# mLSTM values as seven products of halves ahead of the convolutions, with weight sums made by adding DMAs

## The chip, the cores and the metric

The kernel runs on one core of a Trainium2 chip. The metric is the device time of one execution in microseconds (us), the median of several runs; lower is better.

## What is computed

One decoder block on 512 tokens of width 1024. A normalised input `hN` (512 x 1024) is multiplied by one wide matrix whose columns are cut into the inputs of two branches. Branch A is an mLSTM with 4 heads of width 256, branch B a native sparse attention. The outputs of the branches are projected, weighted by the gates `g_a` and `g_b`, added, projected once more, added to `x` and normalised.

```python
hN = _rmsnorm(x, norm_g[l])
p = _split_in(hN @ w_in[l])
mq = jax.nn.silu(_causal_dwconv(p["m_q"], conv_q_w[l], conv_q_b[l]))
mk = jax.nn.silu(_causal_dwconv(p["m_k"], conv_k_w[l], conv_k_b[l]))
mh = _mlstm(mq, mk, p["m_v"], p["m_i"] + b_igate[l], p["m_f"] + b_fgate[l])
mh = _head_layernorm(mh, mh_norm_g[l]).astype(x.dtype)
ya = jax.nn.sigmoid(p["m_o"]) * mh * jax.nn.silu(p["m_z"])
...
yb = yn * jax.nn.silu(p["n_z"])
merged = (jax.nn.sigmoid(p["g_a"]) * (ya @ w_branch_a[l])
          + jax.nn.sigmoid(p["g_b"]) * (yb @ w_branch_b[l]))
x = x + merged @ w_out[l]
```

The part in question is `p["m_v"] = hN @ w_in[:, 2048:3072]`, the values of the mLSTM: 512 tokens by 1024 columns, summed over 1024.

## The kernel before

**Precision.** Each f32 operand is split in a high part, rounded to a shorter format, and a low part, the rest. A product of two f32 blocks takes three matmuls: high by high, high by low, low by high. The transposed input lies in `hTh` and `hTl` (128 partitions, 8 blocks of the summed dimension, 512 tokens). `weights(src)` (lines 155 to 161) fetches 512 KB of weights into `wr` by a DMA issued on SP, copies them to `wh` on ACT and subtracts on DVE to get `wl`; `split` (line 144) does both; every ACT, DVE and POOL operation of the kernel is recorded at line 93, inside a wrapper.

**The stream of jobs.** Weight products are jobs of one queue, `Stream`. A job has a `load` (its call of `weights`) and a generator that issues one matmul at each step. The stream keeps two jobs loaded ahead of the running one. Matmuls of the attention and of the mLSTM heads are written into the program between steps of the stream (`stream.step(6)` and the like), so that TensorE (PE) has projection work while a softmax or a normalisation runs on other engines. The program's order fixes the order on each engine; engines run in order and wait for each other through semaphores.

**Kinds of jobs.** A `cols` job makes 128 columns for all 512 tokens: 8 blocks x 3 passes = 24 matmuls of 128x512 into a PSUM bank `pp`. Its `post` follows on ACT and DVE: for a convolution (`conv`) one ACT operation and three DVE operations for the four taps, a tanh, a product, and a split into `qkh` and `qkl`; for a merge gate one tanh into a tile `s`.

**Order after the attention.** When the attention has ended (its pools are given back), the stream holds: `convs(0)` (4 jobs), `values(0)` (4 jobs), convolutions of head 1, values of the other half, convolutions of heads 2 and 3, and eight gate jobs between and behind them. The first 8 of these jobs, `convs(0)` and `values(0)`, run at once (`stream.run(8)`), and then the loop over four heads begins: each head makes a decay matrix from `ghl` and `sel`, multiplies queries by keys (`qkh`, `qkl`), multiplies by the values (`yah`, `yal`), normalises, and takes steps of the stream between these. `values(half)` (lines 1095 to 1128) makes 512 of the 1024 value columns in four quarters of the summed dimension; a quarter has 4 token blocks x 2 blocks of the sum x 3 passes = 24 matmuls of 128x512, on the banks `ps` and `pt`.

**The tail.** Behind the heads come the six remaining gate jobs, for each of eight blocks of columns a product with `w_branch_a` (24 matmuls) and one with `w_branch_b` (12), and the last projection, which is already done in seven products of halves (Strassen's algorithm) with the tiles `T`, `m11` and `mx2`.

Of the kernel before, what the change touches and what calls it, by code (L numbers as in the profile page):

```python
# [26 lines left out]
START_FILL = 12  # L27
LAG = 3
EARLY = 2
AHEAD = 8  # L30
NORM_FILL = 30

MQ, MK, MV, MO, MZ, MI = 0, 1024, 2048, 3072, 4096, 5120
# [44 lines left out]
def build(  # L78
# [39 lines left out]
    def f(ap):  # L118
        return ap.bitcast(F32)
# [55 lines left out]
    class Stream:  # L175
# [45 lines left out]
    def cols(c0, post, parts=1):  # L221
        def gen(w):
            ps = PP()
            n = T // parts
            for i in range(parts):
                ts = slice(i * n, i * n + n)
                yield from passes(
                    ps[:, ts], lambda k: w[0][:, k, :], lambda k: w[1][:, k, :],
                    lambda k: hTh[:, k, ts], lambda k: hTl[:, k, ts], ND,
                )  # L230
                if i < parts - 1:
                    yield
            post(ps)

        stream.add(lambda: wcols(c0), gen)
# [334 lines left out]

    def gate_ab(base, j, pl):
        def post(ps):
            s = pl.tile([128, T], F32, name="s", tag="s", bufs=EARLY if pl is ybp else AHEAD)
            A(s, ps, AF.Tanh, scale=0.5)
            halves[base, j] = s

        cols(base + j * 128, post)
# [485 lines left out]
        pool.memset(f(vals(h)[:, :, 256:257]), 1.0)  # L1063
        pool.memset(f(vals(h)[:, :, 257:258]), 0.0)

    sgp = ctx.enter_context(tc.tile_pool(name="sgp", bufs=4))
    mlp = tc.tile_pool(name="ml", bufs=1)
    mp = mlp.__enter__()
    later_only = cst[:, CDM : CDM + 128].unsqueeze(1).broadcast_to([128, NT, 128])
    qk, done = {}, set()  # L1070

# [20 lines left out]

        cols((MQ, MK)[i] + (h * 2 + e) * 128, post)

    def values(half):
        banks = []

        def gen(q):
            def run(w):
                if q == 0:  # L1100
                    banks.extend((PS(), PT(), PS(), PT()))
                for tb in range(NT):
                    ts = slice(tb * 128, tb * 128 + 128)
                    ps = banks[tb]
                    for j in range(2):
                        k = 2 * q + j
                        a, b = hTh[:, k, ts], hTl[:, k, ts]
                        pe.matmul(ps, a, w[0][:, j], start=k == 0, stop=False)  # L1108
                        yield
                        pe.matmul(ps, a, w[1][:, j], start=False, stop=False)  # L1110
                        yield
                        pe.matmul(ps, b, w[0][:, j], start=False, stop=k == ND - 1)  # L1112
                        if j == 0:
                            yield
                    if q == 3:
                        hs = slice(2 * half, 2 * half + 2)
                        hi = yah[:, hs, tb * 258 : tb * 258 + 256]
                        lo = yal.rearrange("p (h e) t -> p h (e t)", h=4)
                        lo = lo[:, hs, tb * 256 : tb * 256 + 256]
                        split(ps.rearrange("p (h d) -> p h d", h=2), hi, lo)  # L1120
                    if tb < NT - 1:
                        yield

            return run

        c0 = MV + half * 512
        for q in range(4):
            stream.add(lambda q=q: weights(wv[:, 2 * q : 2 * q + 2, c0 : c0 + 512]), gen(q))

    later = [(base, j) for j in range(ND) for base in (GA, GB)][EARLY:]  # L1130
    ahead = deque(later[:AHEAD])

    def gates_ahead(n):
        for _ in range(n):
            gate_ab(*ahead.popleft(), sgp)
# [12 lines left out]
    gates_ahead(1)  # L1148
    convs(2)
    values(1)  # L1150
    convs(3)
    gates_ahead(4)
    stream.run(8)

    for h in range(4):
        (qh, ql), (kh, kl) = qk[0, h], qk[1, h]
# [72 lines left out]
        while h < 3 and h + 1 not in done:  # L1229
            stream.step(1)  # L1230
        if h < 3:
            stream.run((1, 4, 1)[h])

    mlp.__exit__(None, None, None)
    gtp.__exit__(None, None, None)
# [1 line left out]
    with tc.tile_pool(name="fin", bufs=1) as fp:  # L1237
# [10 lines left out]
        wbv = w_branch_b[0].rearrange("(k p) c -> p k c", p=128)  # L1248
        wov = w_out[0].rearrange("(k p) c -> p k c", p=128)
        L, R = slice(0, 512), slice(512, D)  # L1250

# [21 lines left out]

        def gate_into(base, j, dst):
            halves[base, j] = dst
            cols(base + j * 128, lambda ps: A(dst, ps, AF.Tanh, scale=0.5))
# [15 lines left out]
        def branch(base, j, yh, yl, nk):  # L1292
            def gen(w):
                o = 0 if nk == ND else (j % 2) * 128
                ps = PP()
                yield from passes(
                    ps, lambda k: w[0][:, k, o : o + 128], lambda k: w[1][:, k, o : o + 128],
                    yh, lambda k: yl[:, k], nk,
                )
                s = halves[base, j]  # L1300
                dve.scalar_tensor_tensor(s, s, 1.0, ps, OP.add, OP.mult)
                if base == GB:
                    t = halves.pop((GA, j))
                    dve.tensor_tensor(t, t, halves.pop((GB, j)), OP.add)
                    if j < 4:
                        split(t[:, :256], m11[0][:, j], m11[1][:, j])
                    else:
                        split(t, mx2[0][:, j - 4], mx2[1][:, j - 4])
                    me[j] = t
                    if j > 3:  # L1310
                        sums(j - 4)

            def load():
                if nk == ND:
                    return weights(wav[:, :, j * 128 : j * 128 + 128])
                if j % 2 == 0:
                    halves["w"] = weights(wbv[:, :, j * 128 : j * 128 + 256])
                return halves["w"]

            stream.add(load, gen)  # L1320

        for i, (base, j) in enumerate(later[AHEAD:]):
            gate_into(base, j, fp.tile([128, T], F32, name="g", tag="g", bufs=6))
            if i in (1, 3):
                combine(i // 2)
        for j in range(ND):
            branch(GA, j, ya, yal, ND)
            branch(GB, j, lambda k: ybh[:, k], ybl, 4)

        xo, fg = {}, {}  # L1330

        def fetch_x():
            for hf in (1, 0):
                hs = slice(hf * 512, hf * 512 + 512)
                for tb in range(NT):
                    t = sgp.tile([128, 512], F32, name="s", tag="s", bufs=AHEAD)
# [130 lines left out]
        def after5(l):  # L1467
            partway(2 + l, Z()[l], 1)
# [114 lines left out]
```

## Time and profile before

| what | value |
|---|---|
| median of 3 runs | 628.36 us (628.16 to 628.82) |
| span of the profiled execution, first to last instruction | 626.6 us |
| median above that span | 1.7 us |
| matmuls on PE | 3057 |
| weight loads into PE (PEld), busy | 82% |
| ScalarE (ACT), busy | 50% |
| GpSimd (POOL), busy | 12% |
| data moved by DMA | 60.79 MB, mean 97 GB/s |

The profile records one execution; its time outside the span is not recorded, so the difference to the median stands for it. How to read it: a matmul of 128x512 is listed with a length of 0.39 us, but matmuls are pipelined, and the next one starts 0.23 us later. The pitch, from start to start, is what one matmul costs. An engine's busy share says little by itself; where an engine waits, and for whom, is in the views that list the waits.

### The profile page before, as it was taken

Reading aid. Unit: us, or ns where it says so; the run is one execution under the profiler, and the core shown is the slowest. Engines: PE = TensorE matmul, PEld = TensorE weight load, DVE = VectorE, ACT = ScalarE, POOL = GpSimd, SP = SyncE. Lnnn points to the kernel's source line nnn. Section 1 sums busy time; section 2 is a strip of 40 time slices with the busy share of each in tenths; the row PEclk is TensorE's granted clock in tenths of the full one; section 3 lists DMA queues with packets and bytes.
Section 4 is the critical chain, followed back from the end, with each engine's and each line's share of the span. In section 5 each row is a group of like instructions: output and inputs, shape, how many; then the busy total and the mean of one; then the engine's idle time right before and its main releaser. Section 6 shows DMA issues by size and latency. Waiting matters only on the chain.

```text
span 626.6 us, 8445 instructions
## 1 busy us (share of the span) xinstructions
PE 614.9 (98%) x3057; PEld 512.4 (82%) x3057; DVE 428.7 (68%) x838; ACT 314.1 (50%) x605; POOL 76.4 (12%) x159
## 2 busy tenths in 40 slices
PE   8999999999999999999999999999999999999995
PEld 6988888888788888778888888888888888888884
DVE  4877776876866856758468868656875624578985
ACT  5675556556556656545354554344553232234654
POOL 6220012212221321300000000000000000000013
PEclk9999999999999999999999999999999999999998
DMA  8647532212221122123322322331422752333403
GB/s 284 173 113 186 133 85 67 69 43 59 69 68 51 51 69 67 35 71 98 102 67 68 100 68 69 100 101 33 101 68 67 236 167 86 101 117 101 167 35 134
DMA packets 88602, 60.79 MB, mean 97 GB/s; under 512 B 2881, under 2 KB 79845, under 8 KB 88561
## 3 DMA queue, kind: packets, MB, share of 16 engines
q1 hardware_dynamic: 87982, 59.21, 33.1%
q10 hardware_dynamic: 578, 1.05, 0.5%
q8 instruction: 24, 0.39, 0.3%
q14 instruction: 18, 0.14, 0.1%
HBM read 57.10 MB, written 2.10 MB: 94 GB/s over the span
## 4 chain that ended last, share of the span: by engine, by line
PE 53%; DVE 2%; POOL 1%; ACT 1%; issue 1%; ACTq 0%; DVEq 0%; POOLq 0%
PE pp L213 12%; PE pp L217 12%; PE pp L215 12%; PE pt L1110 1%; PE ps L1110 1%; PE pt L1108 1%; PE ps L1112 1%; PE ps L1108 1%; PE pt L1112 1%; DVE s L93 1%; PE ps L173 1%; PE ps L172 1%; PE ps L171 1%; PE pt L1197 1%; PE pt L1195 1%; PE pt L1196 1%
## 5 line engine op out<-in xcount | busy, mean ns | idle before, releaser
L213 PE MATMUL pp<-hTh,wh 128*128 128x512 f32 (+1 forms) x488 | 191.8, 393 | 0.0
L215 PE MATMUL pp<-hTl,wh 128*128 128x512 f32 (+1 forms) x488 | 191.1, 391 | 0.0
L217 PE MATMUL pp<-hTh,wl 128*128 128x512 f32 (+1 forms) x488 | 190.6, 391 | 0.0
L93 DVE TENSOR_TENSOR wl<-wr,wh 128x1024 fp32r<-128x1024 f32 x86 | 106.0, 1235 | 59.5 <-ACT wh L93 58.4
L93 ACT ACTIVATE wh<-wr 128x1024 fp32r<-128x1024 f32 x86 | 90.9, 1058 | 83.7 <-PE pp L215 52.5
L217 PEld LDWEIGHTS pp<-hTh,wl 128*128 128x128 f32 x488 | 91.9, 188 | 16.6
L213 PEld LDWEIGHTS pp<-hTh,wh 128*128 128x128 f32 x488 | 92.0, 188 | 15.7
L215 PEld LDWEIGHTS pp<-hTl,wh 128*128 128x128 f32 x488 | 92.0, 189 | 15.3
L93 POOL TENSOR_SCALAR P<-P,st,gates 128x128 f32<-128x128 f32 (+1 forms) x64 | 45.3, 722 | 186.3 <-DVE st L93 136.1
L93 ACT ACTIVATE P<-P,st 128x128 f32<-128x128 f32 (+3 forms) x64 | 35.8, 559 | 37.9 <-DVE st L93 37.6
L93 DVE CUSTOM_DVE_ANT_0 P<-ps,cst 128x128 f32<-128x128 f32 (+3 forms) x64 | 30.5, 486 | 22.9 <-PE ps L938 21.8
L93 ACT ACTIVATE pth<-pt 128x512 fp32r<-128x512 f32 (+1 forms) x64 | 26.9, 435 | 28.9 <-PE pt L954 22.2
L93 DVE TENSOR_TENSOR ptl<-pt,pth 128x512 fp32r<-128x512 f32 (+1 forms) x64 | 30.1, 483 | 14.4 <-ACT pth L93 14.0
L93 DVE SCALAR_TENSOR_TENSOR u<-pp,prm,u 128x511 f32<-128x511 f32 (+2 forms) x48 | 35.7, 744 | 0.7
L93 ACT ACTIVATE th<-u 128x512 f32<-128x512 f32 x16 | 10.1, 631 | 41.5 <-DVE u L93 41.5
L954 PE MATMUL pt<-cst,P 128*128 128x128 f32 x160 | 28.9, 277 | 1.6 <-POOL P L93 1.0
L954 PEld LDWEIGHTS pt<-cst,P 128*128 128x128 f32 x160 | 20.1, 141 | 11.7 <-DVE ptl L93 4.9
L93 POOL TENSOR_TENSOR rlr<-va,mhalf 128x4 f32<-128x4 f32 x4 | 4.1, 1020 | 197.0 <-DVE va L93 197.0
L213 PE MATMUL pp<-yah,wh 128*128 128x512 f32 x64 | 24.9, 389 | 0.0
L215 PE MATMUL pp<-yal,wh 128*128 128x512 f32 x64 | 24.9, 389 | 0.0
L217 PE MATMUL pp<-yah,wl 128*128 128x512 f32 x64 | 24.9, 389 | 0.0
L967 PE MATMUL po<-ptl,vsw 128*128 128x512 f32 (+1 forms) x64 | 21.2, 332 | 0.0
(349 smaller groups left out, 1087.0 us busy)
## 6 DMA issues: line engine op xcount, KB each, us to landing
wr<-w_in SPq DMA_DIRECT2D x68, 512.0 KB, 3.9
wr<-w_out SPq DMA_DIRECT2D x8, 512.0 KB, 3.8
wr<-w_branch_a SPq DMA_DIRECT2D x8, 512.0 KB, 3.8
T<-w_out SPq DMA_DIRECT2D x4, 512.0 KB, 6.6
wr<-w_branch_b SPq DMA_DIRECT2D x4, 512.0 KB, 3.6
s<-x SPq DMA_DIRECT2D x8, 256.0 KB, 3.6
xt<-x SPq DMA_DIRECT2D x3, 512.0 KB, 6.1
sraw<-w_small SPq DMA_DIRECT2D x4, 288.0 KB, 5.2
```

Of the source, the lines that this page charges most:

```text
L93: ins = fn(*args, **kw)
L171: pe.matmul(ps, a, c, start=start and i == 0, stop=False)
L172: pe.matmul(ps, a, d, start=False, stop=False)
L173: pe.matmul(ps, b, c, start=False, stop=stop and i == n - 1)
L213: pe.matmul(ps, a, c, start=k == 0, stop=False)
L215: pe.matmul(ps, a, d, start=False, stop=False)
L217: pe.matmul(ps, b, c, start=False, stop=k == nk - 1)
L954: pe.transpose(pt[:, (qb - kb) * 128 : (qb - kb) * 128 + 128], P[:, POFF[qb] + kb * 128 : POFF[qb] + kb * 128 + 128], ident,)
L967: pe.matmul(po[:, kb * 128 :], vl, tl[:, :n], start=False, stop=False)
L1108: pe.matmul(ps, a, w[0][:, j], start=k == 0, stop=False)
L1110: pe.matmul(ps, a, w[1][:, j], start=False, stop=False)
L1112: pe.matmul(ps, b, w[0][:, j], start=False, stop=k == ND - 1)
```

## The change

**Seven products.** The values are the product of `hN` (512 tokens x 1024) and the weights W (1024 x 1024), each cut into two by two quarters of 256 tokens or 512 rows and columns. In place of eight products of quarters there are seven, of sums of quarters. `sum_of_h(n)` makes the sums on the side of `hN` on DVE, from high and low parts added up again, and splits them anew into tiles `S`. The sums on the side of the weights are made by DMA: two tiles `E` of 1 MB each are loaded on SP with a plain DMA in two pieces of 512 KB, and then DMAs issued on POOL with `accum_op=add` (helper `onto`, line 1098) add other quarters of W on top. `E[0]` is W00+W01, later reloaded as W01+W11; `E[1]` is W00+W01+W11 (two adds to each piece), later with W10 added (a third). There are ten adding DMAs of 512 KB. Such a DMA waits until the one before it on the same piece has landed.

**Order.** The seven products are fourteen jobs of 12 matmuls ("strips", two to a product). They come first after the attention, ahead of the convolutions, behind two gate jobs (`FIRST = 2`, 24 matmuls each). The strips' order is: two products of unsummed quarters (`of_h(0)` with W00, `of_h(1)` with W10), then the products `first_sum` (`E[0]`), `second_sum` (`E[1]`), `last_quarter` (W11, unsummed), `third_sum` (`E[0]` reloaded) and `fourth_sum` (`E[1]` with W10). Three partial results leave PSUM to SBUF and come back; PSUM accumulates the others.

**Elsewhere.** Then `convs(0)` and, without values between, the heads. The convolutions of each later head bring two gate jobs along, six in all; with the two first ones that is eight ahead of the tail, and six stay in the tail, as before. The jobs with `w_branch_b` leave the tail and run as the stream's last jobs, in the last head; the product with the gate happens there. The tail makes `w_branch_a` products and adds.

```diff
-AHEAD = 8
+FIRST = 2
+AHEAD = 6
...
+    def onto(e, q, i, j, add=True):
+        if add:
+            nc.gpsimd.dma_start(piece_of(E[e], q), piece_of(wq[i][j], q), accum_op=OP.add)
+        else:
+            nc.sync.dma_start(piece_of(E[e], q), piece_of(wq[i][j], q))
+
+    for q in range(2):
+        onto(0, q, 0, 0, False)
+        onto(0, q, 0, 1)
+    for q in range(2):
+        onto(1, q, 0, 0, False)
+        onto(1, q, 0, 1)
+        onto(1, q, 1, 1)
+    gates_ahead(2, sg0)
...
+    def first_sum(q):
+        w = halves_of(piece_of(E[0], q))
+        if q:
+            E[0] = st.tile([128, 4, 512], F32, name="E", tag="E0")
+            for i in range(2):
+                onto(0, i, 0, 1, False)
+                onto(0, i, 1, 1)
+        return w
+
+    def second_sum(q):
+        w = halves_of(piece_of(E[1], q))
+        onto(1, q, 1, 0)
+        return w
...
+    def strip_product(lhs, load, bank, first, post, pre=((), ())):
+        def gen(q):
+            def run(w):
+                for n in pre[q]:
+                    sum_of_h(n)
+                for l in range(2):
+                    ps = bank(l)
+                    for j in range(2):
+                        a, b = lhs(2 * q + j, l)
+                        c, d = w[0][:, j], w[1][:, j]
...
+    sum_of_h(1)
+    strip_product(of_h(0), from_w(0, 0), X, True, after1, ((), (2,)))
+    strip_product(of_h(1), from_w(1, 0), X, False, lambda l: store_values(l, 0, X(l)), ((3,), (0,)))
+    strip_product(of_sum(1), first_sum, V, True, after5)
+    strip_product(of_sum(2), second_sum, Y, False, after6, ((4,), ()))
+    strip_product(
+        of_sum(3), last_quarter, V, False, lambda l: store_values(l, 1, negated(V(l), kept["p12"][:, l]))
+    )
+    strip_product(
+        of_sum(4), third_sum, Y, False, lambda l: store_values(2 + l, 1, negated(Y(l), kept["p22"][:, l]))
+    )
+    strip_product(of_h(3), fourth_sum, Y, False, lambda l: store_values(2 + l, 0, Y(l)))
...
     convs(0)
-    values(0)
-    convs(1)
-    gates_ahead(1)
-    convs(2)
-    values(1)
-    convs(3)
-    gates_ahead(4)
-    stream.run(8)
+    stream.run(2 + 14)
...
+    for h in range(1, 4):
+        convs(h)
+        gates_ahead(1, sgp)
+    for j in range(ND):
+        branch_b(j)
+    stream.run(4)
```

**POOL's queue**, from the end of the attention to the first head's normalisation (`P`: attention, `yah`: the constant columns of the values, `rlr`: the first normalisation). Before:

```order
L93 TENSOR_SCALAR P<-P,st,gates 128x512
L93 MEMSET yah 128x4 x8
L93 TENSOR_TENSOR rlr<-va,mhalf 128x4 x4
```

With the change:

```order
L94 TENSOR_SCALAR P<-P,st,gates 128x512
L94 MEMSET yah 128x4 x8
L1100 DMA E<-w_in 128x2x512 x10
L94 TENSOR_TENSOR rlr<-va,mhalf 128x4 x4
```

All ten adding DMAs stand in a row on POOL, so an add that must wait holds up those behind it, and the last of them the first head's normalisation.

**SP's queue**, in the same place; each row is a run of DMA issues, and a `wr` tile of 128x2x512 is a piece of a quarter of W, one of 128x8x128 the weights of a `cols` job. Before:

```order
L158 DMA wr<-w_in 128x8x128 x23
L158 DMA wr<-w_in 128x2x512 x4
L158 DMA wr<-w_in 128x8x128 x11
L158 DMA wr<-w_in 128x2x512 x4
L158 DMA wr<-w_in 128x8x128 x11
L1254 DMA wr<-w_out 128x2x512
```

With the change:

```order
L159 DMA wr<-w_in 128x8x128 x21
L159 DMA wr<-w_in 128x2x512 x4
L1102 DMA E<-w_in 128x2x512 x4
L159 DMA wr<-w_in 128x2x512 x2
L159 DMA wr<-w_in 128x8x128
L1102 DMA E<-w_in 128x2x512 x2
L159 DMA wr<-w_in 128x8x128 x21
L159 DMA wr<-w_branch_b 128x4x256 x4
```

The loads of the unsummed quarters stand ahead of the first four loads of `E`, so they can run during the attention's end. The loads of `E` stand between them and the last quarter's.

**DVE's queue**, from the last operation of the attention on (`ybl`; `r_...` are tiles of sums of `hN`, `S_...` their low parts). Before:

```order
L93 TENSOR_TENSOR ybl<-oc,ybh 128x512
L93 TENSOR_TENSOR wl<-wr,wh 128x1024
L93 SCALAR_TENSOR_TENSOR u<-pp,prm,u 128x511
L93 SCALAR_TENSOR_TENSOR u<-pp,prm,u 128x510
L93 SCALAR_TENSOR_TENSOR u<-pp,prm,u 128x509
L93 SCALAR_TENSOR_TENSOR u<-th,u 128x512
```

With the change:

```order
L94 TENSOR_TENSOR ybl<-oc,ybh 128x512
L94 TENSOR_TENSOR r_3022<-hTh,hTl 128x1024
L94 TENSOR_TENSOR r_3023<-hTh,hTl 128x1024
L94 TENSOR_TENSOR wl<-wr,wh 128x1024
L94 TENSOR_TENSOR r_3023<-r_3023,r_3022 128x1024
L94 TENSOR_TENSOR r_3024<-hTh,hTl 128x1024
L94 TENSOR_TENSOR r_3025<-hTh,hTl 128x1024
L94 TENSOR_TENSOR S_3005<-r_3023,S_3004 128x1024
L94 TENSOR_TENSOR wl<-wr,wh 128x1024
L94 SCALAR_TENSOR_TENSOR r_3023<-r_3023,r_3024 128x1024
L94 TENSOR_TENSOR wl<-wr,wh 128x1024
L94 SCALAR_TENSOR_TENSOR r_3025<-r_3023,r_3025 128x1024
```

The convolution's operations have left this place, and operations of twice their width stand there: the sums of `hN` and the splits of the weights.

More of the change, by code (lines that the diff above doesn't have):

```diff
@@ L572, in post @@
         def post(ps):
-            s = pl.tile([128, T], F32, name="s", tag="s", bufs=EARLY if pl is ybp else AHEAD)
+            s = pl.tile([128, T], F32, name="s", tag="s", bufs=AHEAD if pl is not ybp and pl is not sg0 else 2)
             A(s, ps, AF.Tanh, scale=0.5)
@@ L1064, in build, with gates_ahead @@
         pool.memset(f(vals(h)[:, :, 257:258]), 0.0)
-    sgp = ctx.enter_context(tc.tile_pool(name="sgp", bufs=4))
-    mlp = tc.tile_pool(name="ml", bufs=1)
-    mp = mlp.__enter__()
+    sg0 = ctx.enter_context(tc.tile_pool(name="sg0", bufs=1))
+    in_turn = [j for i in range(4) for j in (i, i + 4)]
+    later = [(GB, 1), (GA, 4)] + [(GB, j) for j in range(2, ND)] + [(GA, j) for j in in_turn[2:]]
+    ahead = deque(later[: FIRST + AHEAD])
+    def gates_ahead(n, pl):
+        for _ in range(n):
+            gate_ab(*ahead.popleft(), pl)
@@ new lines, in quarter, with raws, sum_tiles @@
+    def quarter(t, i):
+        ks, ts = slice(4 * (i % 2), 4 * (i % 2) + 4), slice(256 * (i // 2), 256 * (i // 2) + 256)
+        return t[:, ks, ts]
+    stp = tc.tile_pool(name="stp", bufs=1)
+    st = stp.__enter__()
+    def raws(i, shape, name):
+        return st.tile([128, *shape], F32, name=name, tag=f"r{i}")
+    def sum_tiles(n):
+        return [st.tile([128, 4, 256], F32R, name=f"S{n}{i}", tag=f"S{n % 3}{i}") for i in range(2)]
+    S = {n: sum_tiles(n) for n in (1, 2, 3)}
+    E = [st.tile([128, 4, 512], F32, name="E", tag=f"E{i}") for i in range(2)]
@@ new lines, in build, with piece_of @@
+    wq = [
+        [wv[:, 4 * i : 4 * i + 4, MV + 512 * j : MV + 512 * j + 512] for j in range(2)] for i in range(2)
+    ]
+    def piece_of(src, q):
+        return src[:, 2 * q : 2 * q + 2]
+    def onto(e, q, i, j, add=True):
[6 more added lines that the diff above has]
+        onto(0, q, 0, 1)
@@ new lines, in build, with whole_h, sum_of_h @@
+    for q in range(2):
[3 more added lines that the diff above has]
+    gates_ahead(2, sg0)
+    a21, a22, a11, a12 = whole = [raws(i, (4, 256), f"r{i}") for i in range(4)]
+    def whole_h(r, i):
+        dve.tensor_tensor(r, f(quarter(hTh, i)), f(quarter(hTl, i)), OP.add)
+    def sum_of_h(n):
+        if n == 1:
+            whole_h(a21, 2)
+            whole_h(a22, 3)
+            dve.tensor_tensor(a22, a22, a21, OP.subtract)
+            split(a22, *S[1])
+        elif n == 2:
+            whole_h(a11, 0)
+            dve.scalar_tensor_tensor(a22, a22, -1.0, a11, OP.mult, OP.subtract)
+            split(a22, *S[2])
+        elif n == 3:
+            whole_h(a12, 1)
+            dve.scalar_tensor_tensor(a12, a22, -1.0, a12, OP.mult, OP.subtract)
+            split(a12, *S[3])
+        elif n == 0:
+            dve.tensor_tensor(a21, a11, a21, OP.subtract)
+        else:
+            S[4] = sum_tiles(4)
+            split(a21, *S[4])
@@ new lines, in of_h, with get, of_sum, store_values @@
+    def of_h(i):
+        k0, t0 = 4 * (i % 2), 256 * (i // 2)
+        def get(k, l):
+            ts = slice(t0 + l * 128, t0 + l * 128 + 128)
+            return hTh[:, k0 + k, ts], hTl[:, k0 + k, ts]
+        return get
+    def of_sum(n):
+        return lambda k, l: [t[:, k, l * 128 : l * 128 + 128] for t in S[n]]
+    def store_values(tb, half, src):
+        hs = slice(2 * half, 2 * half + 2)
+        hi = yah[:, hs, tb * 258 : tb * 258 + 256]
+        lo = yal.rearrange("p (h e) t -> p h (e t)", h=4)[:, hs, tb * 256 : tb * 256 + 256]
+        split(src.rearrange("p (h d) -> p h d", h=2), hi, lo)
@@ new lines, in build, with bank_of, partial_of, from_w @@
+    kept = {}
+    def bank_of(name, alloc, l):
+        if (name, l) not in kept:
+            kept[name, l] = alloc()
+        return kept[name, l]
+    X, Y, V = [lambda l, n=n, a=a: bank_of(n, a, l) for n, a in (("X", PS), ("Y", PP), ("V", PT))]
+    def partial_of(name, i):
+        if name not in kept:
+            kept[name] = raws(i, (2, 512), name)
+        return kept[name]
+    def from_w(i, j):
+        return lambda q: weights(piece_of(wq[i][j], q))
+    def halves_of(raw):
+        hi = wp.tile([128, 2, 512], F32R, name="wh", tag="wh", bufs=3)
+        lo = wp.tile([128, 2, 512], F32R, name="wl", tag="wl", bufs=3)
+        split(raw, hi, lo)
+        return hi, lo
@@ new lines, in first_sum, with last_quarter, third_sum @@
+    def first_sum(q):
[10 more added lines that the diff above has]
+        return w
+    def last_quarter(q):
+        return from_w(1, 1)(q)
+    def third_sum(q):
+        return halves_of(piece_of(E[0], q))
@@ new lines, in fourth_sum @@
+    def fourth_sum(q):
+        return halves_of(piece_of(E[1], q))
+    def strip_product(lhs, load, bank, first, post, pre=((), ())):
[8 more added lines that the diff above has]
+                        c, d = w[0][:, j], w[1][:, j]
+                        begin = first and q + j == 0
+                        pe.matmul(ps, a, c, start=begin, stop=False, skip_group_check=not first)
+                        yield
+                        pe.matmul(ps, a, d, start=False, stop=False, skip_group_check=not first)
+                        yield
+                        pe.matmul(ps, b, c, start=False, stop=q + j == 2, skip_group_check=not first)
+                        if l + j < 2:
+                            yield
+                    if q == 1:
+                        post(l)
+            return run
+        for q in range(2):
+            stream.add(lambda q=q: load(q), gen(q))
@@ L1093, in conv @@
         cols((MQ, MK)[i] + (h * 2 + e) * 128, post)
[L1095 to L1135, printed above, removed]
     def convs(h):
@@ L1141, in convs, with branch_b, gen, load @@
             if i == 0 and h:
-                gates_ahead(1)
+                gates_ahead(1, sgp)
     convs(0)
-    values(0)
-    convs(1)
-    gates_ahead(1)
-    convs(2)
-    values(1)
-    convs(3)
-    gates_ahead(4)
-    stream.run(8)
+    stream.run(2 + 14)
+    stp.__exit__(None, None, None)
+    sgp = ctx.enter_context(tc.tile_pool(name="sgp", bufs=1))
+    mlp = tc.tile_pool(name="ml", bufs=1)
+    mp = mlp.__enter__()
+    wbv = w_branch_b[0].rearrange("(k p) c -> p k c", p=128)
+    def branch_b(j):
+        def gen(w):
+            o = (j % 2) * 128
+            ps = PP()
+            yield from passes(
+                ps, lambda k: w[0][:, k, o : o + 128], lambda k: w[1][:, k, o : o + 128],
+                lambda k: ybh[:, k], lambda k: ybl[:, k], 4,
+            )
+            s = halves[GB, j]
+            dve.scalar_tensor_tensor(s, s, 1.0, ps, OP.add, OP.mult)
+        def load():
+            if j % 2 == 0:
+                halves["w"] = weights(wbv[:, :, j * 128 : j * 128 + 256])
+            return halves["w"]
+        stream.add(load, gen)
+    for h in range(1, 4):
+        convs(h)
+        gates_ahead(1, sgp)
+    for j in range(ND):
+        branch_b(j)
+    stream.run(4)
     for h in range(4):
@@ L1231, in build @@
         if h < 3:
-            stream.run((1, 4, 1)[h])
+            stream.run()
     mlp.__exit__(None, None, None)
@@ L1247, in build @@
         wav = w_branch_a[0].rearrange("(k p) c -> p k c", p=128)
-        wbv = w_branch_b[0].rearrange("(k p) c -> p k c", p=128)
         wov = w_out[0].rearrange("(k p) c -> p k c", p=128)
@@ L1275, in gate_into @@
             halves[base, j] = dst
-            cols(base + j * 128, lambda ps: A(dst, ps, AF.Tanh, scale=0.5))
+            cols(base + j * 128, lambda ps: left.popleft() and A(dst, ps, AF.Tanh, scale=0.5))
         me = {}
@@ L1290, in sums, with branch_a @@
             split(s34, hTh[:, 2 * i + 1], hTl[:, 2 * i + 1])
-        def branch(base, j, yh, yl, nk):
+        def branch_a(j):
             def gen(w):
-                o = 0 if nk == ND else (j % 2) * 128
                 ps = PP()
                 yield from passes(
-                    ps, lambda k: w[0][:, k, o : o + 128], lambda k: w[1][:, k, o : o + 128],
-                    yh, lambda k: yl[:, k], nk,
-                )
[L1300 to L1328, printed above, removed]
+                    ps, lambda k: w[0][:, k], lambda k: w[1][:, k], ya, lambda k: yal[:, k], ND
+                )
+                t = halves.pop((GA, j))
+                dve.scalar_tensor_tensor(t, t, 1.0, ps, OP.add, OP.mult)
@@ new lines, in gen @@
+                dve.tensor_tensor(t, t, halves.pop((GB, j)), OP.add)
+                if j < 4:
+                    split(t[:, :256], m11[0][:, j], m11[1][:, j])
+                else:
+                    split(t, mx2[0][:, j - 4], mx2[1][:, j - 4])
+                me[j] = t
+                for i in range(4):
+                    if not left and i in me and i + 4 in me:
+                        sums(i)
+            stream.add(lambda: weights(wav[:, :, j * 128 : j * 128 + 128]), gen)
+        turns = deque(in_turn)
@@ L1330, in build @@
+        left = deque(later[FIRST + AHEAD :])
+        n = 0
+        while turns:
+            if left_to_add := later[FIRST + AHEAD + n : FIRST + AHEAD + n + 1]:
+                gate_into(*left_to_add[0], fp.tile([128, T], F32, name="g", tag="g", bufs=6))
+                if n in (1, 3):
+                    combine(n // 2)
+                n += 1
+                if n < 3:
+                    continue
+            branch_a(turns.popleft())
         xo, fg = {}, {}
@@ L1335, in fetch_x @@
                 for tb in range(NT):
-                    t = sgp.tile([128, 512], F32, name="s", tag="s", bufs=AHEAD)
+                    pl, n = (sg0, FIRST) if hf and tb < FIRST else (sgp, AHEAD)
+                    t = pl.tile([128, 512], F32, name="s", tag="s", bufs=n)
                     nc.sync.dma_start(t, x[0, tb * 128 : tb * 128 + 128, hs])
```

9 lines of the change are left out of this document (added).

## The prediction

> **What bounds the kernel now.** I read the busy shares and the granted clock first, then the list of PE's waits.
>
> ```profile
> PE 614.9 (98%) x3057; PEld 512.4 (82%) x3057; DVE 428.7 (68%) x838; ACT 314.1 (50%) x605; POOL 76.4 (12%) x159
> PEclk9999999999999999999999999999999999999998
> PE ps L316 <- DMA grow<-norm_g: 2.2, 1, 2.2
> PE pt L954 <- POOL P L93: 1.0, 2, 0.6
> PE pt L954 <- DVE ptl L93: 0.6, 2, 0.3
> PE po L966 <- ACT pth L93: 0.3, 1, 0.3
> ```
>
> PE works 614.9 of 626.6 us at the full clock, and its waits add up to 4.1 us, all of them ahead of the stage in question: 2.2 at the start, 1.9 in the attention (lines 954 and 966). So the kernel is a gapless row of matmuls, and two questions decide: how many matmuls go, and whether the change opens a gap. The stretch of the values in the timeline of PE (start, length; first and last of the 96 matmuls, and the one after) and the busy time by ten microseconds (PE, PEld, DVE, ACT, POOL, clock, DMA share, GB/s):
>
> ```profile
> 294.60 0.39 PE L1108 MATMUL ps<-wh,hTh 128*128 128x512 f32 x1
> ...
> 316.13 0.39 PE L1112 MATMUL pt<-wh,hTl 128*128 128x512 f32 x1
> 316.36 0.40 PE L1160 MATMUL ps<-ghl,sel 128*128 128x512 f32 x1
> 280.00:290.00 10.00, 10.00 (x46) 8.28 (x45) 7.81 (x11) 3.95 (x6) 0.00 (x0) 1.00 0.37 107
> 290.00:300.00 10.00, 10.00 (x46) 8.29 (x45) 8.77 (x12) 4.77 (x8) 0.00 (x0) 1.00 0.36 103
> 300.00:310.00 10.00, 10.00 (x45) 8.26 (x45) 3.75 (x4) 2.98 (x4) 0.00 (x0) 1.00 0.27 68
> 310.00:320.00 10.00, 10.00 (x45) 7.99 (x43) 6.33 (x8) 6.30 (x13) 0.00 (x0) 1.00 0.32 93
> ```
>
> The 95 steps from 294.60 to 316.13 give a pitch of 0.2266 us. DVE is at 8.8 of 10 us beside the convolutions and at 3.8 beside the values; DMA is at a third.
>
> **What goes from PE.** Before, the values take 2 halves x 4 quarters x 24 = 192 matmuls; now 7 products x 2 strips x 12 = 168, of the same size and with one weight load each, as before. The other products keep their number, since the branch B jobs (8 x 12 matmuls) take the place of four gate jobs (4 x 24) in the last head. That is 24 x 0.2266 = **-5.44 us**, all of it on the path, since PE has no gap there.
>
> **When the sums are wanted.** I keep before's clock: behind the attention, PE's first job starts at 272.84.
>
> ```profile
> 272.84 0.39 PE L213 MATMUL pp<-hTh,wh 128*128 128x512 f32 x1
> 277.15 0.69 DVE L93 TENSOR_TENSOR ybl<-oc,ybh 128x512 fp32r<-128x512 f32 x1 [0.70 <-ACT ybh L93]
> L93 DVE TENSOR_TENSOR wl<-wr,wh 128x1024 fp32r<-128x1024 f32 x86 | 106.0, 1235 | 59.5 <-ACT wh L93 58.4
> L93 ACT ACTIVATE wh<-wr 128x1024 fp32r<-128x1024 f32 x86 | 90.9, 1058 | 83.7 <-PE pp L215 52.5
> ```
>
> Two gate jobs (48 x 0.2266 = 10.88) reach to 283.72; then comes a strip each 2.72 us. I number them from 0: strips 4 and 5 (`first_sum`) start at 294.60, strip 6, the first on `E[1]`, at 300.04, strip 7 at 302.76, strip 10 (`third_sum`) at 310.9. Ahead of a strip lie a copy on ACT (1.06) and a subtraction on DVE (1.23), so the first piece of `E[1]` must have landed at 297.75. The tiles `E` lie in memory that the attention gives back; the last DVE operation on it, `ybl`, ends at 277.84, and SP can't issue the first load of `E` earlier. That leaves 19.9 us for everything up to the fifth add, which completes the first piece of `E[1]`.
>
> **What the adds take.** No adding DMA and no DMA issued on POOL stands in the trace of before. The nearest rows are the plain loads of 512 KB, alone and in a burst of four behind another (issues on SP, the page's median from issue to landing, and two windows of the burst):
>
> ```profile
> wr<-w_in SPq DMA_DIRECT2D x68, 512.0 KB, 3.9
> T<-w_out SPq DMA_DIRECT2D x4, 512.0 KB, 6.6
> 486.28 0.37 SPq L1261 DMA_DIRECT2D T<-w_out  x1
> ...
> 487.72 0.47 SPq L1262 DMA_DIRECT2D T<-w_out  x1
> 486.00:491.60 5.60, 5.60 (x27) 4.63 (x26) 1.42 (x2) 1.54 (x2) 0.00 (x0) 1.00 0.88 254
> 491.60:495.50 3.90, 3.90 (x19) 3.24 (x18) 3.34 (x3) 0.60 (x1) 0.00 (x0) 1.00 1.02 346
> ```
>
> With the DMA engines full (share 1.02) they moved 346 GB/s, so 512 KB (524,288 bytes) take 1.52 us of all engines, and a lone load's 3.9 us holds 2.4 us of latency. Up to the fifth add the engines have four loads of `E`, two `wr` pieces of the unsummed last quarter, and five adds: 11 transfers. If an add costs f times a plain load, the fifth has landed after 6 x 1.52 + 5 x 1.52 f + 2.4 us, and PE is late by that less 19.9: 7.6 (f - 1) - 0.8.
>
> - f = 1: 19.1 of 19.9 us, hidden. But the margin holds no wait of one add for the landing of another (the fifth for the third, in one queue with all others). I take **+0.6**.
> - Lower bound: nothing. An add moves at least a load's bytes, so f is at least 1, and a gain on PE is excluded.
> - Upper bound: if no add overlapped another, five in a row would follow the first load's 3.9 us. At 3.9 each, 23.4 us, 3.5 late; at the burst's 6.6 each, 36.9 us, 17 late.
>
> I take f near 1, since the row of a single load of these bytes is the nearest, and the same bytes come from the same memory. Behind strip 7 each further add has more room: the reload of `E[0]` needs to be ready at 308.6, and its transfers can start once strip 5's split is done, near 296.
>
> The Trainium skill speaks against this value: in "Collectives: The Full Stack", section "The bandwidth ceiling: the fold count and why AG ≠ RS ≠ AR", an addition in the DMA costs nothing as such, but needs two source reads on the same ring, with a measured ratio of 1.93 between plain and adding transfers. By that f would be 1.93, PE 6.3 us late and the time an estimated 629.9 us; no run so far shows it. The same outcome, as a mechanism of this kernel, is the first rival.
>
> **DVE.** From `ybl` (277.84) to strip 6's `wl`, DVE now has 17 operations of 128x1024 (sums of `hN`, their splits, and the `wl`s of strips 1 to 6) and two half as wide. By the row of `wl` that is at most 17 x 1.235 + 2 x 0.69 = 22.4 us, which ends at 300.2 where 300.04 is wanted. Adjacent ones overlap a little, so it may be 1.5 us less. I take **+0.3**; bounds 0 and 2 us (each operation a tenth slower).
>
> **The handover to the first head.** Before, four jobs of values lay between `convs(0)` and the first head, 21.8 us; now none does. The convolution's chain behind its last matmul, for the third and fourth job (whose matmuls end where the next starts, 289.16 and 294.60):
>
> ```profile
> 289.16 0.39 PE L213 MATMUL pp<-hTh,wh 128*128 128x512 f32 x1
> 295.54 0.61 ACT L93 ACTIVATE qkh<-u 128x512 fp32r<-128x512 f32 x1
> 296.81 0.68 DVE L93 TENSOR_TENSOR qkl<-u,qkh 128x512 fp32r<-128x512 f32 x1
> 301.30 0.61 ACT L93 ACTIVATE qkh<-u 128x512 fp32r<-128x512 f32 x1
> 302.57 0.68 DVE L93 TENSOR_TENSOR qkl<-u,qkh 128x512 fp32r<-128x512 f32 x1
> ```
>
> So `qkh` is there 7.0 and 7.3 us after, `qkl` 8.3 and 8.65 us after. Between the third job's end and the first use of its `qkh` the changed order on PE has 31 matmuls (24 of the fourth job, 7 of the next), 7.0 us, and 37 until its `qkl`, 8.4 us: just covered. For the fourth job it has 32 (7.1 us, a few of them narrower) and 36 (7.9 us): 0.2 to 0.7 us short. I take **+0.5**; bounds 0 and 2 us, the latter if DVE is still behind from the strips.
>
> **At no cost.** The three partial results that leave PSUM and come back are ACT and DVE work under strips 8 to 13, where DVE has six `wl` and some ten operations of 0.69 us in 19 us; with that cover gone they would add about 1 us behind the last strip. `w_branch_b` in the last head issues four loads of 512 KB on SP where gate loads stood, with the same matmul time (96 steps) in front. In the tail each `w_branch_a` block has lost the 12 matmuls behind it, 2.7 us of cover for its post, but the next block's 24 follow, 5.4 us. On POOL the last add is queued ahead of the first head's `rlr`, some 20 us later: no wait unless the adds are very late.
>
> **The sum.** -5.44 + 0.6 + 0.3 + 0.5 = -4.0 us on the span of 626.6: 622.6. The median of the runs stands 1.7 us above that span, so the time is **624.3 us**. The likeliest case's own range is 622.9 (nothing but the 24 matmuls) to 626.0 (all three bounded terms larger by 0.6).
>
> **Rivals.**
>
> 1. *The adds cost two transfers* (each reads the weights and the tile that it adds onto). The mechanism sits at strip 6: it waits for the fifth add. With f = 2 PE is late by 6.8 us instead of 0.6, the change gives +2.2, **630.5 us**. It decides from f = 1.72 on, where the delay eats 5.44 - 0.8. With f = 3 it is late by 14.4: 638. For it: DMA is at a third of its time here, and 11 transfers in 19.9 us is near the 1.52 us each that the full engines gave. Against it: the row of a plain load; nothing in the trace tells more.
> 2. *Adds in between* (f 1.3 to 1.9, or one waiting for the other): late by 1.5 to 6.0 us, 625.2 to 629.7.
> 3. *The change doesn't do what it says*: PE does the 24 matmuls less, but waits elsewhere, since DVE, the second busiest, becomes the bound of the strips and the handover takes its 2 us. With both bounds at 2 us and hidden adds, -5.44 + 0.6 + 4 = -0.8: 627.5 at worst, about 626 in the middle.
>
> **How the numbers follow.** The forecast gets 0.43. Rival 3 gets 0.07, all but a trace of it faster. Rival 2 gets 0.17: 0.05 below f = 1.56 and 0.12 above, within 0.2%. Rival 1 gets 0.33: 0.25 up to 632.5 and 0.08 beyond. A measurement can tell about 0.2% (1.25 us) from no change, so faster is below 627.1: 0.43 + 0.07 + 0.05 = 0.55; same 0.12; slower (above 629.6) 0.33. The range, 622.4 to 632.5, reaches to f = 2.25 and leaves out the 0.08 above and little below; with both signs so heavy, it is wide because f is unknown.
>
> **What would show it.** Right: the profile has 3033 matmuls, PE busy some 609.5 us, no wait of PE for `wh<-E` or `wl<-E` above 1 us, and the adds land some 4 us after issue. Wrong by rival 1: PE waits at strip 6 for ACT's `wh<-E`, that waits for a DMA, and the DMA share is near 1 from 278 to 300. Wrong by rival 3: PE waits for a `wl` whose DVE row has no idle time ahead of it, or for `qkh` and `qkl` in the first head.

## The result, and the profile after

| | before | with the change |
|---|---|---|
| median | 628.38 us (4 runs) | 635.28 us (634.82 to 636.86, 4 runs) |
| ratio | 1 | 1.0113, interval 1.0099 to 1.0128 |
| span of the profiled execution | 626.6 us | 634.8 us |

The time is 6.9 us longer, where 4.0 us shorter was forecast. PE does 24 matmuls fewer, as said, and waits. From the page of the changed kernel (the busy times; PE's granted clock; what the queue of POOL's DMAs moved, in MB, and its share of 16 engines' time; the issues of DMAs with their time to landing), and from its list of PE's waits:

```profile
PE 613.4 (97%) x3033; PEld 510.0 (80%) x3033; DVE 450.8 (71%) x860; ACT 326.2 (51%) x621; POOL 89.7 (14%) x169
PEclk9999999999999999999699999999999999999998
q0 software_dynamic: 2720, 5.24, 4.6%
E<-w_in POOLq DMA_DIRECT2D x10, 512.0 KB, 8.7
E<-w_in SPq DMA_DIRECT2D x6, 512.0 KB, 5.6
PE pp L1213 <- ACT wh L94: 8.0, 1, 8.0
PE ps L317 <- DMA grow<-norm_g: 2.6, 1, 2.6
...
PE pp L1215 <- DVE wl L94: 0.5, 1, 0.5
```

There is one new wait of 8.0 us, for a copy on ACT, and one slice of 40 in which the clock is granted only six tenths. An adding DMA takes 8.7 us at the median from issue to landing. Where the wait sits shows in the timeline of PE (start, length, what):

```profile
300.73 0.39 PE L1217 MATMUL pt<-wh,S 128*128 128x512 f32 x1
309.14 0.79 PE L1213 MATMUL pp<-wh,S 128*128 128x512 f32 x1 [8.02 <-ACT wh L94]
310.40 0.79 PE L1215 MATMUL pp<-wl,S 128*128 128x512 f32 x1 [0.47 <-DVE wl L94]
310.99 0.63 PE L1217 MATMUL pp<-wh,S 128*128 128x512 f32 x1
311.42 0.63 PE L1213 MATMUL pp<-wh,S 128*128 128x512 f32 x1
...
316.29 0.40 PE L1213 MATMUL pp<-wh,S 128*128 128x512 f32 x1
```

The last matmul of strip 5 starts at 300.73, so strip 6 was due at 300.96 and starts at 309.14, 8.2 us late. Behind the wait the matmuls follow each other at 0.43 us (310.99 to 311.42) where 0.23 is the rule, up to about 315.7. Who held up strip 6 is in the chain of waits that ended last, followed back through this stretch (start, length, what):

```profile
278.07 0.70 DVE ybl L94
...
278.85 3.81 DMA E<-w_in
...
283.31 2.33 POOL E L1100 x2
285.64 12.82 DMA E<-w_in
...
298.76 9.19 DMA E<-w_in
...
308.03 1.06 ACT wh L94
...
309.12 1.23 DVE wl L94
...
310.40 0.79 PE pp L1215
```

It is the chain of rival 1: `ybl` frees the memory, the first load of `E` is issued, the third add on POOL (issued at 285.64) lands 12.8 us later, and only then is the fifth issued, which lands 9.2 us later, at 307.95. From the end of `ybl` (278.77) to there are 29.2 us. The sum over PE's starts in this stretch, each against the usual pitch: 8.2 us ahead of strip 6, 1.4 until its third matmul, 2.3 in the slow ones behind, 0.5 ahead of strip 12: 12.4 us, less 5.44 is 6.9.

What is left open by this trace: whether the adds' bytes on the DMA engines make the chain long, or the way over POOL's queue with one add waiting for another; how much of the loss is the slow clock; and whether the rest of the change costs something too.

### The profile page after: what moved, and what is told of

It reads as the page before. It is cut to its first block, busy times and chain, and to the rows that moved or that the text cites. A ratio compares the mean times of both kernels' runs of the same rounds, so it can differ in the third digit from the quotient of the medians.

```text
span 634.8 us, 8493 instructions
## 1 busy us (share of the span) xinstructions
PE 613.4 (97%) x3033; PEld 510.0 (80%) x3033; DVE 450.8 (71%) x860; ACT 326.2 (51%) x621; POOL 89.7 (14%) x169
## 3 DMA queue, kind: packets, MB, share of 16 engines
q0 software_dynamic: 2720, 5.24, 4.6%
## 4 chain that ended last, share of the span: by engine, by line
PE 47%; DMA 4%; DVE 3%; ACT 1%; POOL 1%; issue 1%; ACTq 0%; POOLq 0%; SPq 0%; DVEq 0%
PE pp L216 12%; PE pp L214 12%; PE pp L218 12%; DMA E<-w_in 4%; DVE wl L94 1%; PE ps L174 1%; DVE s L94 1%; PE pp L1215 1%; PE pp L1213 1%; PE ps L173 1%; PE ps L172 1%; PE pp L1217 1%; PE pt L1360 1%; PE pt L1362 1%; PE pt L1361 1%
## 5 line engine op out<-in xcount | busy, mean ns | idle before, releaser
L94 DVE TENSOR_TENSOR wl<-wr,wh 128x1024 fp32r<-128x1024 f32 x84 | 103.4, 1233 | 38.0 <-ACT wh L94 36.7
L94 ACT ACTIVATE wh<-wr 128x1024 fp32r<-128x1024 f32 x84 | 88.8, 1058 | 72.3 <-PE pp L216 47.4
```

What stands on the lines that cost most here:

```text
L94: ins = fn(*args, **kw)
```

## Experiments

Each kernel ran beside the kernel before on the same chip; the ratios are to that. Strips are numbered as in the prediction.

### 1. Plain copies on POOL in place of the adds

```diff
-            nc.gpsimd.dma_start(piece_of(E[e], q), piece_of(wq[i][j], q), accum_op=OP.add)
+            nc.gpsimd.dma_start(piece_of(E[e], q), piece_of(wq[i][j], q))
```

> The ten DMAs issued on POOL are plain copies, with the same waits, so the weight sums are not formed (the last quarter copied stands in their place). Theory A (an add costs the DMA engines two reads, 178 ns for a 2 KB packet where a plain one takes 86): packets back at about 86 ns, the fifth DMA on POOL lands some 7 to 8 us earlier, the wait of 8.0 us at strip 6 shrinks to under 2 us, time 624 to 627 us. Rival B (the way over POOL's queue, issue to first packet, and the wait of one add for another's landing set the end, not the bytes): the wait stays over 5 us, time above 631 us.

Measured: 626.19 us (ratio 0.9963, 0.9949 to 0.9977). Its page has this row for POOL's DMAs, and its list of PE's waits (in the stretch from 272 to 340 us) these two:

```profile
q0 software_dynamic: 1440, 5.24, 2.4%
PE pp L1215 <- DVE wl L94: 1.0, 2, 0.8
PE pp L1213 <- DVE p L94: 0.2, 1, 0.2
```

The same 5.24 MB take 2.4% of the engines' time where the adds took 4.6%: by 10 DMAs and the two spans (623.4 and 634.8 us), 1.5 us of all 16 engines for a plain copy and 2.9 us for an add, a ratio of 1.95. The order in POOL's queue and what each DMA waits for are the same, and the wait of 8.0 us is gone: by the landings in the trace, the fifth DMA is there 20.4 us after the end of `ybl`, not 29.2. That is theory A; rival B would have kept the wait.

Two more things differ between the runs. A DMA's issue occupies POOL for 0.7 us, not 1.2 or more, and there are half as many packets (1440, not 2720), since those of the plain copies hold 4 KB and those of the adds 2 KB. The packets' size isn't the cause of the ratio: in the trace of the changed kernel, plain 2 KB packets of SP's queue take 84 ns at the median and the adds' 178 ns; the plain 4 KB packets here take 168 ns.

The Trainium skill gives a ratio of 1.93 ("Collectives: The Full Stack", "The bandwidth ceiling: the fold count and why AG ≠ RS ≠ AR"), measured between AllGather, which copies, and ReduceScatter, which adds, and explains it by two source reads of an add. The 1.95 here agrees with that ratio; that an add reads twice is not shown by any run here.

### 2. Eight products, the rest of the change kept

```diff
-    sum_of_h(1)
-    strip_product(of_h(0), from_w(0, 0), X, True, after1, ((), (2,)))
...
+    values(0)
+    values(1)
...
-    stream.run(2 + 14)
+    stream.run(2 + 8)
```

The tiles `E` and `S` and all adds go with it.

> The eight products of quarters (192 matmuls) in the place of the seven with all their sums; the rest of the change is kept: two gate jobs first, values ahead of the convolutions, branch B in the last head. Theory A (all of the loss sits in the weight sums and what their wait does to PE): 628.4 us as before, within 1 us. Rival C (the handover to the first head or the moved branch B jobs cost part of it): 630 us or more.

Measured: 629.0 us (ratio 1.0002, 0.9993 to 1.0012); PE has 3057 matmuls again. So the place of the values, the two gate jobs ahead, the direct handover to the first head and branch B in the last head cost nothing that can be measured (the interval is some 0.6 us to either side). Rival C is out; the whole loss sits in the sums.

### 3. Work on PE during the wait

```diff
+                if load is second_sum and q == 0:
+                    idle = PO()
+                    for n in range(36):
+                        pe.matmul(idle, hTh[:, n % 8, :128], hTh[:, n % 8], start=n == 0, stop=n == 35)
```

> As the changed kernel, with 36 matmuls (36 x 0.2266 = 8.2 us) on a spare PSUM bank between strips 5 and 6, whose result nobody reads. Theory A with a clock term (after 8 us without work PE runs 13 matmuls at a pitch of 0.43 instead of 0.23 us, 2.6 us in all): the pitch stays 0.23 behind the wait, time 635.3 - 2.6 = 632.7 us, 632 to 633.5. Rival D (the slow matmuls are no part of the loss, since the second piece of E[1] is late as well and would hold PE up instead): 634.5 to 636 us.

Measured: 634.54 us (ratio 1.0091, 1.0076 to 1.0106), with a granted clock of 0.996 to 0.998 in its four runs, where the changed kernel has 0.988 to 0.990. Its timeline of PE at the place of the wait:

```profile
300.27 8.32 PE L1210 MATMUL po<-hTh 128*128 128x512 f32 x36
308.43 0.45 PE L1217 MATMUL pp<-wh,S 128*128 128x512 f32 x1
309.64 0.50 PE L1219 MATMUL pp<-wl,S 128*128 128x512 f32 x1 [0.77 <-DVE wl L94]
309.98 0.40 PE L1221 MATMUL pp<-wh,S 128*128 128x512 f32 x1
310.22 0.40 PE L1217 MATMUL pp<-wh,S 128*128 128x512 f32 x1
```

The matmuls behind the idle ones follow at 0.24 us: the slow pitch came from the wait, not from what the strip does. In this theory A is right. But the time lies where rival D had put it (634.5 to 636 us), since what the clock gives back is in part waited for elsewhere: PE still waits 0.8 us for strip 6's `wl`, and ahead of strip 12 it now waits 0.7 us for DVE, in place of 0.2. By the ratios (1.0112 for the changed kernel in experiment 5) 1.3 us are gained, with an interval of some 1 us on each of the two ratios, so that the times alone hardly tell it from nothing. By PE's starts, in one profiled execution of each, it is 2.0 us. So the slow clock is part of the loss, with 2.3 us of matmul time in the changed kernel, of which not all came back here.

### 4. The unsummed last quarter ahead of `second_sum`

```diff
-    strip_product(of_sum(2), second_sum, Y, False, after6, ((4,), ()))
-    strip_product(
-        of_sum(3), last_quarter, V, False, lambda l: store_values(l, 1, negated(V(l), kept["p12"][:, l]))
-    )
+    strip_product(of_sum(3), last_quarter, V, False, lambda l: None, ((4,), ()))
+    strip_product(of_sum(2), second_sum, Y, False, after6)
```

(`after6` then also does the `store_values` of the last quarter.)

> The product of the unsummed last quarter runs ahead of second_sum, so that E[1] is wanted 5.4 us later; the result is the same. If only the first piece of E[1] is late: wait 8.0 - 5.4 = 2.6 us, most of the clock loss gone, time 635.3 - 5.4 - 2 = 627 to 628 us. Theory A carried on (ten adds at 2.9 us of all engines each, one behind the other from 287 to 321.5 us): the wait moves on to strips 10 to 13, the last of which cannot start before about 325 us instead of 320, time 628 to 630 us.

Measured: 633.33 us (ratio 1.0077, 1.0060 to 1.0093), worse than either expectation. The waits of PE:

```profile
PE pp L1213 <- ACT wh L94: 2.5, 1, 2.5
PE pp L1213 <- DVE p L94: 1.7, 1, 1.7
PE pp L1213 <- ACT p L94: 1.4, 1, 1.4
PE pp L1215 <- DVE wl L94: 0.8, 1, 0.8
```

The wait for `E[1]` fell to 2.5 us, as the first part of the expectation said, but the rest came out otherwise. The clock loss is not gone: behind the waits of 2.5 us and, one matmul later, 0.8 us, eight matmuls (start 311.2 to 314.2) still follow at about 0.43 us. And two more waits stand behind: `third_sum` now follows `second_sum` on the same PSUM bank and waits for ACT to copy it out (1.4), and the last product waits for a subtraction on DVE (1.7) that is queued behind the `wl` of a late sum. The last quarter had been the cover of that bank. Neither part of the expectation had this.

### 5. The changed kernel again

> The changed kernel once more, on the chip of the runs beside it: 635.3 us within 1, granted clock 0.988 to 0.990, one wait of about 8 us at strip 6 and slow matmuls behind it.

Measured: 635.69 us, ratio 1.0112 (1.0097 to 1.0128), clock 0.988, one wait of 7.8 us at strip 6. It serves the runs beside it as their reference.

### 6. One add less in `E[1]`

```diff
         onto(1, q, 0, 1)
-        onto(1, q, 1, 1)
```

> E[1] is made with one add in the place of two to each piece (W11 is left out of it), so that strip 6 waits for the third add on POOL and no longer for the fifth, which waited for the third to land. Theory A (each add takes 2.9 to 3.7 us of all DMA engines here, and a dependent one is issued only after the other's landing): the third add lands at about 298.0 in the changed kernel's clock less the 0.9 us by which it started late, where strip 6 wants it at 297.75; the wait at strip 6 falls from 8.0 to under 1 us and the one at strip 7 (fourth add, landed about 301) to about 1 us; time 624.5 to 627 us. Rival E (the two loads and adds of E[0] ahead of it already fill the time): the wait stays over 3 us, time above 629.

Measured: 630.83 us (ratio 1.0032, 1.0020 to 1.0044). The wait at strip 6 is gone, as theory A said and against rival E; yet the time is above 629 us, which A had not said. The waits of PE from 296 to 330 us, at strip 12 (for `p`), strip 11 (for `wh`) and strips 10 and 11 (for `wl`):

```profile
PE pp L1212 <- DVE p L94: 2.3, 1, 2.3
PE pp L1212 <- ACT wh L94: 2.1, 1, 2.1
PE pp L1214 <- DVE wl L94: 1.0, 2, 0.8
```

The timeline of POOL shows why:

```profile
304.61 4.90 POOL L1100 DMA_DIRECT2D E<-w_in  x4 [15.26 <-DVE wl L94]
```

The last four adds are issued in a row at 304.61, when the reload of `E[0]` has landed (304.05 by its semaphore, issued at 297.75 into full DMA engines). The row names a `wl` on DVE as what ended the wait; it ended at 304.18, and the profile doesn't tell the two apart. The order of the adds is `E[0]`, `E[1]`, `E[0]`, `E[1]`, and they land 3 to 4 us after one another, so that strip 11's sum stands behind one that only strip 12 needs; and DVE, in order, comes to the subtraction `p` that frees strip 12's PSUM bank only behind strip 11's late `wl`. The expectation had looked at the deadlines of strips 6 and 7 alone.

### 7 and 8. Sums on POOL

In experiment 7 `E[0]` keeps its two adds, and the other sums are additions on POOL from raw pieces in `wr`:

```diff
+    def pool_add(e, q, a, b):
+        pool.tensor_tensor(piece_of(E[e], q), a, b, OP.add)
...
+    def second_sum(q):
+        raw11[q] = raw_of(1, 1, q)
+        pool_add(1, q, piece_of(E[0], q), raw11[q])
...
+    def last_quarter(q):
+        w = halves_of(raw11.pop(q))
+        pool_add(1, q, piece_of(E[1], q), raw_of(1, 0, q))
+        return w
```

Experiment 8 makes `E[0]` on POOL too.

> Only E[0] is still made by two adding DMAs. E[1], E[0] reloaded and E[1] with W10 are made by six additions of 128x1024 on POOL from plain loads in wr; the piece of W11 that the last quarter needs anyway serves three sums. The result is the same. Theory A: eight adding DMAs and four loads of E go, three plain loads of W10 and the like stay, so the DMA engines have slack; if a POOL addition takes 2 to 3 us, no strip waits over 1 us, time 628.5 - 5.4 + 1 to 2 = 624 to 625.5 us. Rival F (POOL's additions take over 4 us each, or slow DVE beside them): waits move to strips 6 to 12, time 627 or more.

> As the run with the sums on POOL, and E[0] too is made there, from the loaded W01 and the raw W00 of strips 0 and 1: no adding DMA is left, two loads fewer. Theory A: as e7 or up to 1 us better, 623.5 to 625.5 us. Against it: the raw tiles of W00 are held until POOL has read them, which delays the load of W10's second piece for strip 3; then a wait of 1 to 3 us at strip 3, time 625 to 627.

Measured: 631.91 us (ratio 1.0055, 1.0039 to 1.0072) and 636.03 us (1.0115, 1.0094 to 1.0137). In experiment 7, PE's waits from 272 to 345 us, the timeline of DVE, and the operations on the tiles `E` (duration: least, median, most, in ns):

```profile
PE pp L1221 <- DVE p L94: 2.3, 1, 2.3
PE pp L1223 <- DVE wl L94: 2.1, 3, 1.5
PE pt L1223 <- DVE wl L94: 0.7, 2, 0.4
304.27 1.23 DVE L94 TENSOR_TENSOR S<-r,S 128x1024 fp32r<-128x1024 f32 x1 [0.21 <-ACT S L94]
305.70 6.60 DVE L94 TENSOR_TENSOR wl<-wr,wh 128x1024 fp32r<-128x1024 f32 x2 [0.21 <-ACT wh L94]
312.22 6.75 DVE L94 TENSOR_TENSOR wl<-E,wh 128x1024 fp32r<-128x1024 f32 x2
L94 DVE TENSOR_TENSOR wl<-E,wh x8: 1211/1220/3411, 292.5 to 322.4; 128x1024 fp32r<-128x1024 f32 x8
L94 POOL TENSOR_TENSOR E<-E,wr x6: 2393/3044/9536, 289.8 to 315.2; 128x1024 f32<-128x1024 f32 x6
```

Two operations on DVE take 6.6 us together while POOL adds, where two take 2.4 us otherwise, and single ones up to 3.4 us; POOL's own are listed with 2.4 to 9.5 us. It goes both ways: beside POOL's longest addition, from 289.8 to 299.4, DVE's operations keep their 1.22 us. Rival F, then, by its second half: the two engines hold each other up while both add or subtract two tensors in SBUF (the core's memory beside PSUM), and PE's waits, for DVE throughout, lie at strips 6 to 12 as it said. The Trainium skill says so ("SBUF — State Buffer", "Who interferes with whom": a VectorE operation with two SBUF inputs contends with a GpSimd operation that reads SBUF), and this trace agrees.

Experiment 8 is slower than either part of its expectation. The first of POOL's additions run beside DVE's sums of `hN`, of which two now take 6.77 us:

```profile
282.41 6.77 DVE L94 TENSOR_TENSOR r<-hTh,hTl 128x1024 f32<-128x1024 f32 x2
PE ps L1220 <- ACT pp L94: 2.1, 2, 1.3
PE ps L1222 <- DVE wl L94: 1.0, 1, 1.0
```

PE waits 3.1 us already in strip 2 (the tile `ps`), for a copy on ACT and a `wl` on DVE that come late, and again in the later strips. No run tells how much of this is DVE's slower pace and how much the loads that wait for POOL to free the raw pieces.

### 9. Sums on DVE

`E[0]` and the last step of `E[1]` keep their four adding DMAs. `E[1]` becomes `E[0]` plus the raw W11, and the reloaded `E[0]` gets the same raw pieces, in four additions on DVE. The difference `a21` is taken one strip later.

```diff
+    def second_sum(q):
+        if q == 0:
+            for i in range(2):
+                raw11[i] = raw_of(1, 1, i)
+                dve.tensor_tensor(piece_of(E[1], i), piece_of(E[0], i), raw11[i], OP.add)
...
+    def third_sum(q):
+        dve.tensor_tensor(piece_of(E[0], q), piece_of(E[0], q), raw11[q], OP.add)
+        return halves_of(piece_of(E[0], q))
```

> Six of the ten adding DMAs go: E[1] and the reloaded E[0] are made by four additions of 128x1024 on DVE from W11's raw pieces, which are loaded once for three uses; E[0] and the last step of E[1] keep their four adding DMAs. The result is the same. Theory A (the bytes of the adds on the DMA engines, and what stands behind them in order, make the loss): DVE has 2.0 and 2.7 us idle ahead of the wl of strips 6 and 7 in the run with plain copies, which takes two additions of 1.22 us; no wait of PE over 1 us in the strips, time 624.5 to 626.5 us, faster than before by 2 to 4 us. Rival G (DVE is the bound of the strips already, each of its additions comes on top): 4 x 1.22 = 4.9 us more than the 626.2 of the plain copies, 629 to 631.

Measured: 624.56 us (624.26 to 624.89, 5 runs; ratio 0.9928, 0.9915 to 0.9942). It is 4.4 us faster than before and 11 us faster than the change as made. Beside the six adds it drops two plain loads, so its gain isn't that of the adds alone. PE's waits between 272 and 330 us, in full, and DVE at strip 6:

```profile
PE pp L1219 <- DVE p L94: 0.4, 1, 0.4
296.83 2.35 DVE L94 TENSOR_TENSOR E<-E,wr 128x1024 f32<-128x1024 f32 x2
299.10 1.22 DVE L94 TENSOR_TENSOR r<-r,r 128x1024 f32<-128x1024 f32 x1
300.24 2.35 DVE L94 TENSOR_TENSOR wl<-E,wh 128x1024 fp32r<-128x1024 f32 x2
```

Two additions take 2.35 us on DVE, less than the 2.9 us of one in the DMA engines, and fit where DVE had been idle. Theory A holds; rival G does not.

## Why the prediction was wrong, step by step

- **The 24 matmuls**, -5.44 us: right. PE has 3033, and experiment 9, which waits for next to nothing, gains 4.4 us; small gaps between PE's starts in the strips make up the 1.0 us between.
- **What the adds take** is the step that failed: "I take f near 1, since the row of a single load of these bytes is the nearest, and the same bytes come from the same memory." Only the bytes that arrive from memory were counted. An add takes 1.95 times a plain copy of the same size (experiment 1), 2.9 us of all engines. With f = 1.95 the prediction's own sum has PE late by 6.4 us and gives 630.1 us: this step alone turns the sign.
- **Rival 1** named the mechanism, the place (strip 6, the fifth add) and the sign, but gave 630.5 us; the time lies above the range, in the 0.08 that the prediction had left there. Its sum was short by 4.8 us, in two places.
- **The length of the chain**, 2.5 us: the fifth add landed 29.2 us after `ybl`, where f = 2 gave 26.7. The count of 11 transfers left out three loads that SP's queue moves ahead of that landing, the first weights of the convolutions and the two reloads of `E[0]`. From 278.8 to 308 us the trace of the changed kernel has 4.83 MB on SP's queue, 9.2 loads of 512 KB where six were counted, and 3.02 MB on POOL's; their packets take 48.7% and 56.5% of the 16 engines' time, so the engines were full. At the prediction's 1.52 us three loads are 4.6 us, more than is missing. Besides, the whole chain had one latency of 2.4 us, while it has the first load's landing (3.8), the issue on POOL, and the second add's wait for the first to land. With plain copies, where f is 1, the fifth was there after 20.4 us, where the sum gave 19.1.
- **The price of a wait**, 2.3 us: I had priced the wait of PE at its length alone, and the matmuls at half pace behind it (experiment 3 shows that they come from the wait) were not in it. The Trainium skill has that rule ("TensorE: Matmul & The Clock Gate", "What's actually happening": after about 3.4 us without work the clock goes to half). The trace agrees on the half, with 0.43 for 0.23 us, and the slow stretch lasted about 6.5 us here, from 309.14 to 315.7; but in experiment 4 shorter waits, of 2.5 and 0.8 us with one matmul between them, were enough for eight matmuls at that pace.
- **The margin behind strip 7** ("each further add has more room") was wrong as well, hidden behind the first wait: experiment 6 shows strips 10 to 12 late once strip 6 is not, with 2.1 us for strip 11's `wh` and 2.3 us ahead of strip 12.
- **DVE**, +0.3: about right. With plain copies PE waits 1.0 us for `wl`, but DVE sat idle for 2.0 and 2.7 us ahead of those two `wl`, so that the copies' landing held them up. With four operations more on DVE, placed with care, no wait for a `wl` is listed.
- **The handover**, +0.5: nothing that can be measured. No kernel here shows a wait of PE for `qkh` or `qkl` in the first head, and experiment 2 puts the rest of the change at 1.0002.
- **Rivals 2 and 3**: rival 2 ended at f = 1.9, just under the measured ratio, and its price was too low for the same reasons as rival 1's; rival 3 did not occur.

What isn't settled: how the 2.5 us by which the chain is longer divide between the three loads, the issue on POOL and the landings. No run changed the loads or the queue alone.

## What to carry to other kernels

Price an adding DMA at two transfers of its size, count every transfer that shares the engines until it lands, and follow a chain of dependent ones landing by landing; where an engine has gaps of an operation's length, the same sum can be cheaper there, as two additions on DVE in 2.35 us against 2.9 us of all DMA engines for one. When a wait is moved from one deadline, check all later deadlines of the same queue: the wait at strip 6 hid two more. On PE, the wait of 8 us cost more than 8 us: 2.3 us of matmuls at half pace came on top.

## What the runs showed of the hardware

- Adding DMAs of f32 from memory onto SBUF take 1.95 times the engine time of plain copies from the same queue (4.6% of 634.8 us against 2.4% of 623.4 us for 5.24 MB); by packets of 2 KB it is 178 ns against the 84 ns of a plain load on SP's queue.
- After a wait of 8.0 us on PE some 12 matmuls run at 0.43 instead of 0.23 us; with other matmuls in the wait they don't. After waits of 2.5 and 0.8 us with one matmul between (experiment 4) it is eight.
- An addition of 128x1024 on POOL takes 2.4 us at best, and DVE's operations with two inputs in SBUF beside it go from 1.2 to as much as 3.4 us, or keep their 1.2 while the addition is listed with 9.5.
